# One explicit order of transfers for a residual-add layer norm: 16-row loads, stores ahead of the loads that follow them, finer last blocks

## Chip, cores and metric

The kernel runs on one core of a Trainium2 chip. The metric is device time in microseconds (us) of one execution; lower is better. A profiled execution gives a "span", about 1.3 us shorter than the device time of the same run. DVE is VectorE, ACT is ScalarE, POOL is GpSimd, SP is the sync engine, which issues all large transfers here. A core has 16 DMA engines, and every large transfer is spread over all of them (128 data packets, which the packet records show as 16 chains of 8).

"Row" means below one row of the 512 numbers *in each of the 128 partitions*: 128 x 2 KB = 256 KB. The problem has 128 such rows. So x16+16 is the load of rows 16 to 31 of x, 4 MB; r is the residual and o the output.

## The reference

```python
# x, residual: (16, 1024, 512) float32; gamma ones, beta zeros; eps 1e-5
z = x + residual
mean = np.mean(z, axis=-1, keepdims=True)
var = np.var(z, axis=-1, keepdims=True)
return (gamma * (z - mean) / np.sqrt(var + eps) + beta).astype(np.float32)
```

Each number of x and residual is read once and each of the output written once: 100.66 MB in all, and no order of transfers changes that.

## The kernel before

x is loaded into a ring of 64 rows (zbuf), the residual into a ring of 32 rows (rbuf). POOL adds the residual in place, ACT takes the mean and the sum of squares of each row in groups of four, DVE normalizes in place, and zbuf is stored. SP issues every transfer in one queue, and waits on semaphores where a ring is not yet free. The order of issue comes from a rule:

```python
X_CHUNKS = [8] * 15 + [4, 4]           # R_CHUNKS is the same
OUT_CHUNKS = [16] * 7 + [8, 4, 4]
Z_ROWS = 64; R_ROWS = 32; STORE_LAG = 40; ADD = 8
# ... (cut)
for c, (lo, n) in enumerate(loads_x):
    asked = lo + n
    while stored < asked - Z_ROWS:                 # the ring slot's old rows must be stored
        o = next(i for i, b in enumerate(stores) if b[0] == stored)
        nc.sync.wait_ge(so[o], 16)
        stored += stores[o][1]
    move(part(zbuf, Z_ROWS, lo, n), dram(xf, lo, n), sx[c])
    while todo_r and todo_r[0][1][0] + todo_r[0][1][1] <= asked:
        rc, (rlo, rn) = todo_r.pop(0)
        wait_rows(s_add, "add", rlo + rn - R_ROWS) # the residual slot must have been added
        move(part(rbuf, R_ROWS, rlo, rn), dram(rf, rlo, rn), sr[rc])
    while todo_o and (todo_o[0][1][0] + todo_o[0][1][1] <= asked - STORE_LAG or asked == total):
        oc, (olo, on) = todo_o.pop(0)
        wait_rows(s_out, "out", olo + on)          # the rows must be normalized
        move(dram(of, olo, on), part(zbuf, Z_ROWS, olo, on), so[oc])
# ... (cut: POOL adds each residual chunk, in pieces of ADD rows; ACT and DVE work in groups of 4 rows)
```

## Time and profile before

| | before |
|---|---|
| device time, median (lowest to highest) of the first 3 runs | 239.17 us (239.12 to 239.27) |
| transfers by SP; data packets per DMA engine | 44; 352 |
| share of the DMA engines' time that the packets took | 99.3% |
| ACT, DVE, POOL busy | 78%, 74%, 60% |

These lines are from the page of the kernel before: the span, the engines' busy time with shares, DMA's busy tenths and GB/s in 40 equal slices, the packets, the queue's share of 16 engines, and the chain of work that ended last, by engine and by line.

```profile
span 237.9 us, 1484 instructions
...
PE 3.7 (2%) x4; PEld 1.2 (0%) x4; DVE 177.2 (74%) x290; ACT 185.5 (78%) x545; POOL 142.2 (60%) x21
...
DMA  8999999999999999999999999999999999999996
GB/s 309 441 433 421 433 433 433 419 427 441 421 438 419 438 427 424 468 441 386 427 433 435 441 413 433 430 449 430 413 430 419 457 441 383 455 435 430 421 417 287
DMA packets 6341, 100.68 MB, mean 423 GB/s; under 512 B 706, under 2 KB 706, under 8 KB 708
...
q1 hardware_dynamic: 6336, 100.67, 99.3%
...
DMA 49%; ACT 24%; POOL 11%; DVE 5%; issue 4%; SPq 1%; ACTq 1%; DVEq 0%; POOLq 0%
DMA rbuf<-in_residual_dram 36%; ACT junk_s L211 14%; DMA out_dram<-zbuf 13%; POOL zbuf L181 11%; ACT junk_m L201 10%; DVE zbuf L239 3%; DVE zbuf L251 3%; SPq L138 1%; ACTq L201 1%; DVEq L239 0%; ACT std L220 0%; DVE rstd L248 0%; ACTq L192 0%; ACTq L198 0%; DVEq L231 0%
...
```

How to read them: the DMA row is 9 (90% or more) in every slice but the two at the ends, and the queue's packets took 99.3% of the engines' time. No compute engine is above 78%. The core is bound by its DMA engines, and it moved 423 GB/s over the whole span. The Trainium skill ("HBM Reference", Specifications (TRN2)) says of a core that streams alone that it measures about 425 GB/s, "bounded by its 16 DMA engines"; this trace agrees.

The next two fences show, first, the SP queue's own waits in the kernel before (what waited, for what, us in total, times, longest); second, POOL's adds, with their idle time after the bar.

```profile
engine line waited for: us in total, times, longest us
SPq L138 <- DMA out_dram<-zbuf: 110.5, 4, 29.1
SPq L138 <- DVE zbuf L251: 64.7, 6, 29.0
SPq L138 <- POOL zbuf L181: 33.8, 3, 15.8
...
```

```profile
...
L181 POOL TENSOR_TENSOR zbuf<-zbuf,rbuf 128x4096 f32<-128x4096 f32 (+1 forms) x17 | 142.0, 8353 | 70.6 <-DMA rbuf<-in_residual_dram 70.6
...
```

SP waited 209 us of a span of 238, and POOL 70.6 us for residual loads. Neither is a cost in itself. SP's part of the timeline shows it around the first store:

```profile
...
50.50 0.35 SPq L138 DMA_DIRECT2D out_dram<-zbuf  x1
50.89 0.43 SPq L138 DMA_DIRECT2D zbuf<-in_x_dram  x1
51.37 0.43 SPq L138 DMA_DIRECT2D rbuf<-in_residual_dram  x1
80.94 0.33 SPq L138 DMA_DIRECT2D zbuf<-in_x_dram  x1
...
```

SP stood still from 51.8 to 80.9 us, waiting for the store asked for at 50.5 to land. But an x load and a residual load had been put behind that store. The packet records show the store's last packets ending at 80.0 us at the median engine, and those two loads then keeping it busy until 89.8. SP had asked for the next x load at 80.9, 8.9 us in time.

The trace also holds one record for each packet. One transfer makes 8 data packets on each engine, one for each partition; its packet is as long as its rows in that partition: 8 KB for 4 rows, 16 KB for 8, 32 KB for 16. In the kernel before, packets took at the median 309, 613 and 1213 ns. So 16 KB cost a little more than half of 32 KB.

### The profile page before, as it was taken

The page shows a single profiled execution, that of the slowest core. Times are in us where ns is not written, and L with a number is a line of the kernel's source. Part 1 is how long each engine was busy: PE and PEld are TensorE (multiplying, and loading weights), DVE is VectorE, ACT ScalarE, POOL GpSimd, SP SyncE. Part 2 cuts the span into 40 slices and gives each one's busy share as a digit, 9 for nine tenths or more (in the row PEclk, how much of TensorE's full clock was granted, in tenths as well). Part 3 has the DMA queues.
Part 4 walks back from the last instruction along what each step waited for, and adds up shares of the span by engine and source line. Part 5 has one row for each costly group of instructions (what it writes and reads, how often), then busy time and mean ns, then how long its engine had stood idle before and what let it go on. Part 6 is the DMA issues. An engine that isn't in the chain of part 4 may idle for free.

```text
span 237.9 us, 1484 instructions
## 1 busy us (share of the span) xinstructions
PE 3.7 (2%) x4; PEld 1.2 (0%) x4; DVE 177.2 (74%) x290; ACT 185.5 (78%) x545; POOL 142.2 (60%) x21
## 2 busy tenths in 40 slices
PE   0600000000000000000000000000000000000000
PEld 0100000000000000000000000000000000000000
DVE  0000498989898989898989898963989549898950
ACT  2003999999999999999999999739996399999600
POOL 0098988989889407893078930889209892770000
DMA  8999999999999999999999999999999999999996
GB/s 309 441 433 421 433 433 433 419 427 441 421 438 419 438 427 424 468 441 386 427 433 435 441 413 433 430 449 430 413 430 419 457 441 383 455 435 430 421 417 287
DMA packets 6341, 100.68 MB, mean 423 GB/s; under 512 B 706, under 2 KB 706, under 8 KB 708
## 3 DMA queue, kind: packets, MB, share of 16 engines
q1 hardware_dynamic: 6336, 100.67, 99.3%
q14 instruction: 1, 0.01, 0.0%
q10 hardware_dynamic: 4, 0.00, 0.0%
HBM read 67.11 MB, written 33.55 MB: 423 GB/s over the span
## 4 chain that ended last, share of the span: by engine, by line
DMA 49%; ACT 24%; POOL 11%; DVE 5%; issue 4%; SPq 1%; ACTq 1%; DVEq 0%; POOLq 0%
DMA rbuf<-in_residual_dram 36%; ACT junk_s L211 14%; DMA out_dram<-zbuf 13%; POOL zbuf L181 11%; ACT junk_m L201 10%; DVE zbuf L239 3%; DVE zbuf L251 3%; SPq L138 1%; ACTq L201 1%; DVEq L239 0%; ACT std L220 0%; DVE rstd L248 0%; ACTq L192 0%; ACTq L198 0%; DVEq L231 0%
## 5 line engine op out<-in xcount | busy, mean ns | idle before, releaser
L181 POOL TENSOR_TENSOR zbuf<-zbuf,rbuf 128x4096 f32<-128x4096 f32 (+1 forms) x17 | 142.0, 8353 | 70.6 <-DMA rbuf<-in_residual_dram 70.6
L239 DVE SCALAR_TENSOR_TENSOR zbuf<-zbuf,nm,gamma_p 128x512 f32 x128 | 87.1, 742 | 48.7 <-ACT junk_s L211 48.7
L201 ACT ACTIVATE junk_m<-zbuf 128x512 f32 x128 | 74.8, 585 | 31.5 <-POOL zbuf L181 29.1
L211 ACT ACTIVATE junk_s<-zbuf,nm 128x512 f32 x128 | 88.9, 695 | 1.0
L251 DVE SCALAR_TENSOR_TENSOR zbuf<-zbuf,rstd,beta_p 128x512 f32 x128 | 87.1, 743 | 1.1
L211 ACT ACTIVATION_READ_ACCUMULATOR junk_s<-zbuf,nm 128x1 f32 x128 | 23.9, 187 | 0.0
L201 ACT ACTIVATION_READ_ACCUMULATOR junk_m<-zbuf 128x1 f32 x128 | 23.9, 186 | 0.0
L220 ACT ACTIVATE std<-ssq,eps_t 128x4 f32<-128x4 f32 x32 | 9.5, 297 | 3.0
L248 DVE RECIPROCAL rstd<-std 128x4 f32<-128x4 f32 x32 | 5.4, 170 | 0.0
L189 ACT ACT_TABLE_LOAD x1 | 1.3, 1283 | 2.7 <-PEq L56 2.7
L123 PE MATMUL gamma_p<-gb_row,ones 1*128 1x512 f32 x2 | 2.0, 1118 | 7.2 <-DMA gb_row<-in_gamma_dram 7.2
L123 PE MATMUL beta_p<-gb_row,ones 1*128 1x512 f32 x2 | 1.9, 1052 | 0.0
L118 DVE MEMSET ones<- 1x128 f32 x1 | 0.2, 165 | 2.0 <-PEq L56 2.0
L123 PEld LDWEIGHTS beta_p<-gb_row,ones 1*128 1x128 f32 x2 | 0.7, 328 | 1.0 <-issue 0.5
L123 PEld LDWEIGHTS gamma_p<-gb_row,ones 1*128 1x128 f32 x2 | 0.5, 308 | 7.2 <-issue 7.2
L287 POOL MEMSET const-float32-0.0<- 128x1 f32 x1 | 0.1, 99 | 0.2 <-issue 0.2
L287 POOL MEMSET const-bfloat16-1.0<- 128x1 bf16 x1 | 0.1, 102 | 0.0
L287 POOL MEMSET const-uint8-127<- 128x1 uint8 x1 | 0.1, 102 | 0.0
L287 POOL MEMSET const-float32-1.0<- 128x1 f32 x1 | 0.1, 99 | 0.0
L119 DVE MEMSET eps_t<- 128x1 f32 x1 | 0.1, 59 | 0.0
## 6 DMA issues: line engine op xcount, KB each, us to landing
zbuf<-in_x_dram SPq DMA_DIRECT2D x15, 2048.0 KB, 32.9
rbuf<-in_residual_dram SPq DMA_DIRECT2D x15, 2048.0 KB, 30.1
out_dram<-zbuf SPq DMA_DIRECT2D x7, 4096.0 KB, 28.5
zbuf<-in_x_dram SPq DMA_DIRECT2D x2, 1024.0 KB, 32.5
rbuf<-in_residual_dram SPq DMA_DIRECT2D x2, 1024.0 KB, 34.5
out_dram<-zbuf SPq DMA_DIRECT2D x1, 2048.0 KB, 15.7
out_dram<-zbuf SPq DMA_DIRECT2D x2, 1024.0 KB, 10.4
gb_row<-in_gamma_dram ACTq DMA_DIRECT2D x1, 2.0 KB
```

Source lines behind the costliest of these rows:

```text
L118: nc.vector.memset(ones[:, :], 1.0).then_inc(s_const, 1)
L123: nc.tensor.matmul(dest[:, :], ones[:, :], gb_row[:, k * D : (k + 1) * D], start=True, stop=True).then_inc(s_pe, 1)
L138: i = nc.sync.dma_start(out=out, in_=in_).then_inc(s, 16)
L181: nc.gpsimd.tensor_tensor(out=z, in0=z, in1=part(rbuf, R_ROWS, a, an), op=ALU.add).then_inc(s_add, an)
L189: act.preload_act_table_set("sqrt_and_others")
L201: i = act.activation(out=junk_m[k][:, :], in_=zk[k], func=ACT.Identity, scale=-inv_d, accum_out=nm[j][:, k : k + 1],)
L211: i = act.activation(out=junk_s[k][:, :], in_=zk[k], func=ACT.Square, bias=nm[j][:, k : k + 1], accum_out=ssq[j][:, k : k + 1],)
L220: act.activation(out=std[j][:, :], in_=ssq[j][:, :], func=ACT.Sqrt, bias=eps_t[:, 0:1], scale=inv_d,).then_inc(s_std, TURN)
L239: dve.scalar_tensor_tensor(out=zk[k], in0=zk[k], scalar=nm[j][:, k : k + 1], in1=gamma_p[:, :], op0=ALU.add, op1=ALU.mult,)
L248: dve.reciprocal(out=rstd[j][:, :], in_=std[j][:, :]).then_inc(s_dve, TURN)
L251: i = dve.scalar_tensor_tensor(out=zk[k], in0=zk[k], scalar=rstd[j][:, k : k + 1], in1=beta_p[:, :], op0=ALU.mult, op1=ALU.add,)
L287: nc = _bacc.Bacc("TRN2", target_bir_lowering=False, num_devices=1)
```

## The change

The intent: one list of transfers in place of the rule. Loads take 16 rows where they can, in 32 KB packets; each store is put ahead of the residual and x loads that follow it; the last blocks are finer than 16 rows (x in 8 rows, the last store in 12 and 4), though not finer than in the kernel before, which ends with x loads of 4 and 4 rows and stores of 8, 4 and 4; adds take 4, 4 and 8 rows of each block, so that ACT can start sooner.

```diff
-X_CHUNKS = [8] * 15 + [4, 4]
-R_CHUNKS = [8] * 15 + [4, 4]
-OUT_CHUNKS = [16] * 7 + [8, 4, 4]
+BLOCK = 16
-STORE_LAG = 40
-ADD = 8
+PLAN = """
+x0+8 r0+8 x8+8 r8+8 x16+16 r16+16 x32+16 r32+16
+x48+16 r48+16 o0+16 r64+16 x64+16 o16+16 r80+16 x80+16
+o32+16 r96+16 x96+8 x104+8 o48+16 r112+16 x112+8 x120+8
+o64+16 o80+16 o96+16 o112+12 o124+4
+"""
+ADDS = [4, 4, 8] * 7 + [4] * 4
 # ... (cut: parsing of PLAN; the DRAM view takes blocks of BLOCK rows)
+    for kind, lo, n in moves:
+        if kind == "x":
+            while gone < len(stores) and stores[gone][0] < lo + n - Z_ROWS:
+                nc.sync.wait_ge(so[gone], 16)
+                gone += 1
+            move(part(zbuf, Z_ROWS, lo, n), dram(xf, lo, n), sx[loads_x.index((lo, n))])
+        elif kind == "r":
+            wait_rows(s_add, "add", lo + n - R_ROWS)
+            move(part(rbuf, R_ROWS, lo, n), dram(rf, lo, n), sr[loads_r.index((lo, n))])
+        else:
+            wait_rows(s_out, "out", lo + n)
+            move(dram(of, lo, n), part(zbuf, Z_ROWS, lo, n), so[stores.index((lo, n))])
 # ... (cut: the loop by rule goes; POOL waits for the loads that each piece of ADDS needs)
```

ACT's and DVE's code and the bytes moved stay the same.

More of the change, by code (lines that the diff above doesn't have):

```diff
@@ L56, with of_kind @@
     tc.compile()
-    def spans(sizes):
-        assert sum(sizes) == total
-        return [(sum(sizes[:c]), n) for c, n in enumerate(sizes)]
-    blocks = spans(OUT_CHUNKS)
+    moves = []
+    for word in PLAN.split():
+        kind, (lo, n) = word[0], map(int, word[1:].split("+"))
+        assert lo // BLOCK == (lo + n - 1) // BLOCK
+        moves.append((kind, lo, n))
+    def of_kind(kind):
+        found = [(lo, n) for k, lo, n in moves if k == kind]
+        assert sum(n for _, n in found) == total
+        return found
     def dram(t, lo, n):
-        b0, bn = next(b for b in blocks if b[0] <= lo and lo + n <= b[0] + b[1])
-        v = t[P * b0 : P * (b0 + bn), :].rearrange("(p j) d -> p j d", p=P)
+        b0 = lo - lo % BLOCK
+        v = t[P * b0 : P * (b0 + BLOCK), :].rearrange("(p j) d -> p j d", p=P)
         return v[:, lo - b0 : lo - b0 + n, :].rearrange("p a b -> p (a b)")
@@ L92, in sem @@
         return s
-    loads_x, loads_r, stores = spans(X_CHUNKS), spans(R_CHUNKS), blocks
+    loads_x, loads_r, stores = of_kind("x"), of_kind("r"), of_kind("o")
     sx = [sem(f"sx{c}") for c in range(len(loads_x))]
@@ L125 @@
         ).then_inc(s_pe, 1)
-    todo_r, todo_o = list(enumerate(loads_r)), list(enumerate(stores))
     seen = {"add": 0, "out": 0}
@@ L140, in move @@
             first.append(i.ins)
-    stored = 0
-    for c, (lo, n) in enumerate(loads_x):
-        asked = lo + n
-        while stored < asked - Z_ROWS:
-            o = next(i for i, b in enumerate(stores) if b[0] == stored)
-            assert all(o != t[0] for t in todo_o)
-            nc.sync.wait_ge(so[o], 16)
-            stored += stores[o][1]
-        move(part(zbuf, Z_ROWS, lo, n), dram(xf, lo, n), sx[c])
-        while todo_r and todo_r[0][1][0] + todo_r[0][1][1] <= asked:
-            rc, (rlo, rn) = todo_r.pop(0)
-            wait_rows(s_add, "add", rlo + rn - R_ROWS)
-            move(part(rbuf, R_ROWS, rlo, rn), dram(rf, rlo, rn), sr[rc])
-        while todo_o and (
-            todo_o[0][1][0] + todo_o[0][1][1] <= asked - STORE_LAG or asked == total
-        ):
-            oc, (olo, on) = todo_o.pop(0)
-            wait_rows(s_out, "out", olo + on)
-            move(dram(of, olo, on), part(zbuf, Z_ROWS, olo, on), so[oc])
-    for o, (lo, n) in enumerate(stores[:-1]):
-        if lo >= stored:
-            nc.sync.wait_ge(so[o], 16)
+    gone = 0
+    for kind, lo, n in moves:
[10 more added lines that the diff above has]
+            move(dram(of, lo, n), part(zbuf, Z_ROWS, lo, n), so[stores.index((lo, n))])
+    for o in range(gone, len(stores) - 1):
+        nc.sync.wait_ge(so[o], 16)
     nc.sync.sem_clear(range(nums[0], nums[-1]))
@@ L169 @@
     nc.sync.sem_clear(range(nums[-1], nums[-1] + 1))
-    for c, (lo, n) in enumerate(loads_x):
-        nc.gpsimd.wait_ge(sx[c], 16)
-        for rc, (rlo, rn) in enumerate(loads_r):
-            if lo <= rlo < lo + n:
-                assert rlo + rn <= lo + n
-                nc.gpsimd.wait_ge(sr[rc], 16)
-                for a in range(rlo, rlo + rn, ADD):
-                    an = min(ADD, rlo + rn - a)
-                    z = part(zbuf, Z_ROWS, a, an)
-                    nc.gpsimd.tensor_tensor(
-                        out=z, in0=z, in1=part(rbuf, R_ROWS, a, an), op=ALU.add
-                    ).then_inc(s_add, an)
+    landed = {"x": 0, "r": 0}
+    lo = 0
+    for n in ADDS:
+        for key, loads, s in (("x", loads_x, sx), ("r", loads_r, sr)):
+            while landed[key] < len(loads) and loads[landed[key]][0] < lo + n:
+                nc.gpsimd.wait_ge(s[landed[key]], 16)
+                landed[key] += 1
+        z = part(zbuf, Z_ROWS, lo, n)
+        nc.gpsimd.tensor_tensor(
+            out=z, in0=z, in1=part(rbuf, R_ROWS, lo, n), op=ALU.add
+        ).then_inc(s_add, n)
+        lo += n
+    assert lo == total
     act = nc.scalar
```

## The prediction

> **What bounds the kernel now.** The DMA engines. The page's row of DMA busy tenths is 9 in all slices but the first and last, and its part on DMA queues gives q1 99.3% of the 16 engines' span, at 423 GB/s. The trace's packet records, laid out by engine, show no hole in the middle: first packet about 1.1 us into the span, then back to back (largest hole 0.34 us, on one engine), most engines ending near 236.15 us, and about 1.75 us of receipt and semaphores after. ACT (78%), DVE (74%) and POOL (60%) are not the limit. The sync queue's 110.5 us of waiting for stores, and POOL's 70.6 us for the residual, look like what the change attacks, but earlier transfers fill the DMA engines meanwhile, so this waiting costs nothing. The chain of waits names residual and store transfers because they stand in one full queue.
>
> The Trainium skill ("DMA: Bandwidth & Descriptors", Specifications) gives a fabric ceiling of 435 GB/s. The trace agrees: 32 KB packets of 1213 ns on 16 engines are 432 GB/s. 100.67 MB at 435 GB/s is 231.4 us; with the two ends about 234.3, so there is hardly 2% to win.
>
> **What the change does.** Bytes, DVE and ACT work stay. Transfers fall from 44 to 29, each 8 packets per DMA engine, so packets per engine from 352 to 232. Start to start, before's packets took 309 ns (8 KB), 613.6 (16 KB), 1211 (32 KB): two of 16 KB cost 16 ns more than one of 32 KB.
> Before: 31x8 of 16 KB (152.2) + 7x8 of 32 KB (67.8) + 6x8 of 8 KB (14.8) = 234.8 us; measured about 235.0.
> After: 19x8 of 32 KB (184.1) + 8x8 of 16 KB (39.3) + 8 of 24 KB (7.3, interpolated) + 8 of 8 KB (2.5) = 233.1 us. Gain 1.7 us, if 32 KB loads run as the 32 KB stores do. I take off a little.
>
> POOL has 25 adds in place of 17; two 4-row adds cost 9.06 us, one of 8 rows 8.87. ACT can start near 17 us instead of 21.3. Both off the critical path.
>
> **Does the queue stay fed?** By hand, from 0.613 us per row of transfer, 4.5/8.9 us adds, 5.9 us per 4 rows of ACT: r32 is asked for near 30 us with queued work until 49; r48 and o0 near 58 with work until 69; from x64 on each x load waits for the store 64 rows earlier, with one 16-row residual load (9.8 us) queued behind that store: a margin near 8 us. Loads end near 197; stores o64, o80, o96 hold the queue until 226; rows 124 and 128 are ready near 218 and 224. No hole expected.
>
> **Predicted time.** 239.17 - 1.5 = 237.7 us; 8 in 10 within 237.1 to 238.9. Faster by over 2%: 0.01; within 2%: 0.97; slower by over 2%: 0.02.
>
> **What the profile would show.** Right: about 4,200 packets in place of 6,341; busy tenths still 9 throughout; about 426 GB/s; the sync queue's and POOL's waits still large; last packet to end still near 1.75 us. Wrong: slices below 9 in 90-180 us (an x load asked for too late) or 224-230 us (last rows late), or 32 KB load packets slower than 1213 ns.
>
> **What would make it wrong.** 32 KB load packets much slower or faster than the stores; stores that land over 8 us after their last packet, a hole at every x load; the last 16 rows computed later than reckoned.

## The result and the profile after

| | before | after |
|---|---|---|
| device time, median (lowest to highest), 5 runs each | 239.27 us (239.12 to 239.43) | 238.07 us (238.04 to 238.31) |
| transfers by SP; data packets per DMA engine | 44; 352 | 29; 232 |
| packet time per DMA engine | 235.90 us | 234.80 us |

The ratio is 0.9955, 95% interval 0.9943 to 0.9967: 0.45% faster, well inside 2%, and clear of noise. "Packet time per engine" is the summed duration of all data packets divided by 16. Within a transfer, the records of one engine overlap by 3 to 4 ns, so this sum counts a little time twice: 1.2 us per engine before, 0.8 after.

The same lines of the page, after:

```profile
span 236.9 us, 1471 instructions
...
PE 3.7 (2%) x4; PEld 1.2 (0%) x4; DVE 177.2 (75%) x290; ACT 185.5 (78%) x545; POOL 143.0 (60%) x29
...
DMA  8999999999999999999999999999999999999996
GB/s 310 443 432 426 426 443 443 443 443 443 426 415 398 443 443 443 426 420 409 431 437 443 443 443 432 420 407 429 443 437 437 409 432 448 437 420 437 426 430 285
DMA packets 4181, 100.68 MB, mean 425 GB/s; under 512 B 466, under 2 KB 466, under 8 KB 468
...
q1 hardware_dynamic: 4176, 100.67, 99.2%
...
DMA 71%; POOL 9%; ACT 9%; DVE 2%; issue 2%; SPq 1%; ACTq 0%; DVEq 0%; POOLq 0%
DMA out_dram<-zbuf 49%; DMA rbuf<-in_residual_dram 16%; POOL zbuf L180 9%; DMA zbuf<-in_x_dram 6%; ACT junk_s L212 5%; ACT junk_m L202 4%; SPq L146 1%; DVE zbuf L240 1%; DVE zbuf L252 1%; ACTq L202 0%; DVEq L240 0%; ACT std L221 0%; DVE rstd L249 0%; ACTq L193 0%; POOLq L177 0%
...
```

The DMA row has not changed, there are 4181 packets in place of 6341, and the span is 1.0 us shorter. The chain of work now names stores for 49% where it named residual loads for 36%; in both kernels it only tells which member of one full queue something happened to wait for. SP's own waits and POOL's adds, after:

```profile
engine line waited for: us in total, times, longest us
SPq L146 <- POOL zbuf L180: 94.0, 6, 27.6
SPq L146 <- DMA out_dram<-zbuf: 74.0, 4, 21.0
SPq L146 <- DVE zbuf L252: 46.0, 3, 22.0
...
```

```profile
...
L180 POOL TENSOR_TENSOR zbuf<-zbuf,rbuf 128x2048 f32<-128x2048 f32 (+1 forms) x25 | 142.8, 5740 | 67.6 <-DMA zbuf<-in_x_dram 40.8
...
```

SP's waits sum to 214 us (209 before), and POOL's idle time fell from 70.6 to 67.6 us; POOL now waits for x loads more than for residual loads. All this moved, and none of it is where the 1 us came from. SP's timeline after, around the first store:

```profile
...
59.78 0.43 SPq L146 DMA_DIRECT2D out_dram<-zbuf  x1
78.83 0.33 SPq L146 DMA_DIRECT2D rbuf<-in_residual_dram  x1
90.61 0.33 SPq L146 DMA_DIRECT2D zbuf<-in_x_dram  x1
...
```

x64 is asked for at 90.6 us, when the store o0 has landed; at that moment the residual load r64 is in transfer, and x64's first packet starts at 99.3 at the median engine. The margin is 8.7 us, about as before (8.9).

One thing appears in the packet records that was not there before. At 76 to 79 us, in the last packets of r48, the load ahead of the first store, nearly every engine has slow packets: up to 465 ns over the usual 1213, in sum 0.37 us per engine. If one counts only packets more than 60 ns over the usual time of their size, the excess per engine is 0.69 us before (0.61 of it in the first 2 us) and 1.10 us after. So the shorter packet list saved 1.10 + 0.41 = 1.5 us of summed packet time, and 0.4 us was given back. Another 0.4 us of the 1.5 is only overlap of records that went away (1.2 us before, 0.8 after): from its first packet to its last, the mean engine took 234.9 us before and 234.2 after.

### The profile page after: what moved, and what is told of

Its sections match the earlier page's. It is cut to its first block, busy times and chain, and to the rows that moved or that the text cites. A ratio compares the mean times of both kernels' runs of the same rounds, so it can differ in the third digit from the quotient of the medians.

```text
span 236.9 us, 1471 instructions
## 1 busy us (share of the span) xinstructions
PE 3.7 (2%) x4; PEld 1.2 (0%) x4; DVE 177.2 (75%) x290; ACT 185.5 (78%) x545; POOL 143.0 (60%) x29
## 2 busy tenths in 40 slices
DMA packets 4181, 100.68 MB, mean 425 GB/s; under 512 B 466, under 2 KB 466, under 8 KB 468
## 3 DMA queue, kind: packets, MB, share of 16 engines
q1 hardware_dynamic: 4176, 100.67, 99.2%
## 4 chain that ended last, share of the span: by engine, by line
DMA 71%; POOL 9%; ACT 9%; DVE 2%; issue 2%; SPq 1%; ACTq 0%; DVEq 0%; POOLq 0%
DMA out_dram<-zbuf 49%; DMA rbuf<-in_residual_dram 16%; POOL zbuf L180 9%; DMA zbuf<-in_x_dram 6%; ACT junk_s L212 5%; ACT junk_m L202 4%; SPq L146 1%; DVE zbuf L240 1%; DVE zbuf L252 1%; ACTq L202 0%; DVEq L240 0%; ACT std L221 0%; DVE rstd L249 0%; ACTq L193 0%; POOLq L177 0%
## 5 line engine op out<-in xcount | busy, mean ns | idle before, releaser
L180 POOL TENSOR_TENSOR zbuf<-zbuf,rbuf 128x2048 f32<-128x2048 f32 (+1 forms) x25 | 142.8, 5740 | 67.6 <-DMA zbuf<-in_x_dram 40.8
## 6 DMA issues: line engine op xcount, KB each, us to landing
zbuf<-in_x_dram SPq DMA_DIRECT2D x6, 2048.0 KB, 14.9
```

The costliest lines, as they stand in the source:

```text
L180: nc.gpsimd.tensor_tensor(out=z, in0=z, in1=part(rbuf, R_ROWS, lo, n), op=ALU.add).then_inc(s_add, n)
```

## The experiments

Theory P: the gain is packet overhead only; order matters only in that the queue must never run empty. Rival O: the order of transfers (stores ahead, fewer or shorter waits) is itself worth the time. Runs of one batch share the chip and the runs of the kernel before.

### The changed kernel again

No edit.

> The changed kernel again, so that it stands on the same chip as the next three. Both theories: about 238.1 us, about 1.1 us below the kernel before. Its first profile held one stall of about 0.4 us on all 16 DMA engines near 77 us; if that was chance, this profile shows no such stall, and a span of about 236.7 us.

Measured: 238.26 us (238.08 to 238.51), ratio to before 0.9962 (0.9948 to 0.9976). The stall near 77 us was there again, 0.43 us per engine, and a second small one at 194 us (0.29). The first is no chance; the expectation of a clean profile was wrong.

### Its order, with 8-row loads

```diff
-x0+8 r0+8 x8+8 r8+8 x16+16 r16+16 x32+16 r32+16
+x0+8 r0+8 x8+8 r8+8 x16+8 x24+8 r16+8 r24+8 x32+8 x40+8 r32+8 r40+8
 # ... (all later 16-row loads alike; stores unchanged)
```

> The changed kernel's order, with each 16-row load cut into two of 8 rows (41 transfers, 328 data packets per DMA engine in place of 232). Packet theory (the gain is packet overhead, about 9 to 14 ns for each packet more): slower than the changed kernel by 0.9 to 1.3 us, about 239.1 us. Order theory (the gain is the order of transfers): as the changed kernel, 238.1 us.

Measured: 239.00 us (238.92 to 239.08), ratio to before 0.9994 (0.998 to 1.0007). The changed order, the stores ahead, the finer last blocks and the 4-row adds are all in this kernel, and with 8-row loads together they are worth nothing that can be told from zero. Rival O falls. From its page:

```profile
span 237.7 us, 1488 instructions
...
DMA packets 5909, 100.68 MB, mean 424 GB/s; under 512 B 658, under 2 KB 658, under 8 KB 660
...
q1 hardware_dynamic: 5904, 100.67, 99.3%
...
```

### Its order, with every transfer in pieces of 4 rows

```diff
-x0+8 r0+8 x8+8 r8+8 x16+16 r16+16 ...
+x0+4 x4+4 r0+4 r4+4 x8+4 x12+4 r8+4 r12+4 x16+4 x20+4 x24+4 x28+4 ...
 # ... (all loads and stores alike: 96 transfers)
```

> The changed kernel's order, with every transfer cut into pieces of 4 rows (96 transfers, 768 packets of 8 KB per engine). Packet theory: 768 packets at 306 to 309 ns are 235.3 to 237.3 us where the changed kernel has 233.1, so 2 to 5 us slower than the changed kernel, 240.5 to 243 us. Order theory: 238.1 us, or faster, since waits end on smaller pieces.

Measured: 242.79 us (242.54 to 242.88), ratio to before 1.0148 (1.0134 to 1.0162). From its page:

```profile
span 241.5 us, 1564 instructions
...
DMA packets 13831, 100.70 MB, mean 417 GB/s; under 512 B 1538, under 2 KB 1538, under 8 KB 1540
...
q1 hardware_dynamic: 13824, 100.67, 99.6%
...
```

The engines are even "busier" than before, 99.6%, and the kernel is slower: a busy DMA engine is not one at its best. The three kernels of this batch are a dose and a response, by their means: 232 packets per engine, 238.25 us; 328, 239.00 us; 768, 242.73 us. That is 0.75 us for 96 packets and 3.72 us for 440, so 7.9 and 8.5 ns for each packet more. The kernel before has 352 packets: 24 more than the second, and 239.00 + 24 x 8.5 ns gives 239.2; it measured 239.13. One line runs through four kernels, three with the changed order and one with the old; that is the strongest evidence for theory P.

The slope of that line is not the cost of one packet, however. In the 4-row kernel one engine ended 2.3 us after the median one (241.0 and 238.7 us), in the repeat of the changed kernel 0.8 us after it (236.5 and 235.7), so 1.6 of the 4.5 us between the two profiles come from one late engine; and the 232-packet kernel has the stall, which the other two lack. From start to start, without each kernel's first transfer, packets took 309 ns (8 KB, in the 4-row kernel), 611 (16 KB) and 1212 (32 KB; both in the kernel before): 10 ns for each packet more from 32 to 16 KB, 6 ns from 16 to 8 KB.

Two rivals go along with packet size in these runs. The packet records of the kernel before speak against both. Number of transfers: where a new transfer begins, the next packet starts 6 to 9 ns later than within one, so 15 transfers fewer are worth about 0.1 us (an estimate from these two numbers). Addresses: most 8-row loads read half of each partition's 32 KB in a 16-row block, but x112 and r112 have an 8-row block to themselves and read it whole, and their packets took 614 and 615 ns, like those of the other later 8-row loads (611 to 615).

### The old rule with 16-row loads, nothing else changed

```diff
-X_CHUNKS = [8] * 15 + [4, 4]
-R_CHUNKS = [8] * 15 + [4, 4]
+X_CHUNKS = [8, 8] + [16] * 6 + [8, 4, 4]
+R_CHUNKS = [8, 8] + [16] * 6 + [8, 4, 4]
```

> The kernel before with 16-row loads and nothing else changed: by its rule each store from the first on is now asked for just before the x load that waits for it. Queue theory: four holes of about 2 us, near 246 to 248 us, so larger loads alone are a loss and the order must come with them. If larger loads are all that counts: 238.3 us.

Measured: 252.18 us (251.78 to 252.47), ratio 1.0543. Its page's span and DMA row:

```profile
span 251.1 us, 1466 instructions
...
DMA  8999999999999979999699995999997999999998
...
```

The holes are where they were expected, one before each of x64, x80, x96 and x112, but they cost 13 us in place of 8. Why is taken up at the next run.

### The changed kernel with its stores behind the residual loads

```diff
-x48+16 r48+16 o0+16 r64+16 x64+16 o16+16 r80+16 x80+16
+x48+16 r48+16 r64+16 o0+16 x64+16 r80+16 o16+16 x80+16
 # ... (o32 and o48 alike)
```

> The changed kernel with each store from o0 to o48 moved behind the residual load that followed it, so that nothing is queued behind the store for whose landing the next x load waits. Theory that the order matters only in that it keeps the queue from running empty: four holes of about 2 us (0.8 us from the last packet to the next ask, 1.2 us from the ask to the first packet), 246 to 248 us, and a slice below 9 tenths at each. Theory that the queue has enough in it in any order: 238.1 us.

Measured: 253.18 us (253.08 to 253.60), ratio 1.059. From its page:

```profile
span 251.8 us, 1471 instructions
...
DMA  8999999999999999699996999969999799999998
GB/s 328 422 429 487 416 416 416 427 479 427 416 416 364 453 349 416 250 422 474 354 416 250 448 458 344 416 250 437 479 333 437 268 419 375 422 437 448 432 411 350
DMA packets 4181, 100.68 MB, mean 400 GB/s; under 512 B 466, under 2 KB 466, under 8 KB 468
...
q1 hardware_dynamic: 4176, 100.67, 96.5%
...
```

The bytes and packets are the same as in the changed kernel; the queue's share fell from 99.2% to 96.5%, and the DMA row dips at each store. SP's timeline at the first one, and the window of that hole (us; each engine's busy time; granted clock, DMA share, GB/s):

```profile
...
78.86 0.33 SPq L146 DMA_DIRECT2D rbuf<-in_residual_dram  x1
79.23 0.43 SPq L146 DMA_DIRECT2D out_dram<-zbuf  x1
102.01 0.33 SPq L146 DMA_DIRECT2D zbuf<-in_x_dram  x1
...
```

```profile
...
101.00:104.00 3.00, 0.00 (x0) 0.00 (x0) 2.77 (x5) 2.88 (x11) 0.00 (x0) 1.00 0.62 175
...
```

The store o0 is asked for at 79.2, and x64, which needs its ring slot, next, with nothing queued between. The store's packets end at 101.1 us at the median engine and 101.7 at the last, SP asks for x64 at 102.0, and its first packet starts at 103.1 at the median engine. The hole is 2.0 us, as expected: 0.9 from the median last packet to the ask, 1.1 from the ask to the first packet. The five gaps (0.4 us before r64, then 1.7 to 2.0 us after each of the four stores, means over the engines) sum to 7.7 us per engine. The Trainium skill ("DMA: Bandwidth & Descriptors", Anatomy of one DMA) gives a fixed cost of about 2.0 us for a DMA, most of it completion, for another issue path; a cost of that size is what shows here once nothing hides it, but in other parts: 1.1 of the 2.0 us lie between the ask and the first packet, and of the 0.9 us before the ask 0.6 is the wait for the last engine.

The other half had not been foreseen. After each hole, packets were slow: in the first packets after the restart (0.64 to 0.69 us per engine, as much as the 0.69 us of this kernel's own start), and again at the end of the loads, just ahead of the next store (0.85 to 1.1 us per engine). By the count of packets over 60 ns late, the excess is 9.2 us per engine, against 1.5 in the repeat of the changed kernel. Gaps of 7.7 and 7.7 us of excess make 15.4 us, and the median engine does end 15.4 us later than in that repeat (251.1 and 235.7 us). The spans differ by 251.8 - 236.9 = 14.9, because the last engine ends 0.3 us after the median here and 0.8 us after it there. So the size that was wrong is settled: an empty queue costs not only its gap but about as much again in slow packets after it. What makes the packets ahead of the next store slow was not found.

So the order is worth a great deal in one sense: 16-row loads need it. With the old rule they cost 13 us; with the list they save 1.

### The old rule with 16-row loads and stores asked for 8 rows sooner

```diff
 # the chunk lists as in the old rule with 16-row loads above
-STORE_LAG = 40
+STORE_LAG = 32
```

> The kernel before with its own rule of order, x before residual, only with 16-row loads, and stores asked for 8 rows earlier so that there is still a load behind each store (32 transfers, 256 packets per engine). Packet theory: nearly all of the gain, about 238.3 us. Order theory: no gain, about 239.2 us.

Measured: 245.65 us (245.47 to 246.25), ratio 1.0279. Both expectations missed. From its page:

```profile
span 244.2 us, 1466 instructions
...
DMA  8999999999999999999999999999999999989574
...
q1 hardware_dynamic: 4608, 100.67, 96.5%
...
```

There is no hole at the x loads: the lag did what it was chosen for. The holes are in the last slices. With x96 and r96 as one transfer each, POOL could begin on row 96 only at 178.2 us, when all of r96 had landed; in the kernel before it began at 159.4, in the changed one at 163.4. ACT takes 5.9 us for four rows, so the last 32 rows take it 47 us, and the stores of the last blocks were asked for at 216.4, 228.4, 234.5 and 240.3 us, each after its predecessor had ended at the median engine. The gaps before them there are 1.1, 2.2, 1.2 and 3.3 us: 7.8 us, against 7.4 us between this kernel's time and the changed one's (238.26 in the same batch). So this run does not speak about packets or order in the middle; it shows the second thing that an order must do: bring the last rows in early enough. That is what the split of x96 and x112 in the list was meant for; that the split itself is needed is not shown. In the kernel with two pairs of transfers merged (below), x96 is one load of 16 rows in the changed order: POOL began on row 96 at 168.8 us, and no hole came of it.

### Adds of 8 rows

```diff
-ADDS = [4, 4, 8] * 7 + [4] * 4
+ADDS = [8] * 15 + [4, 4]       # first kernel
+ADDS = [8] * 14 + [4] * 4      # second kernel
```

> The changed kernel with adds of 8 rows and 4, 4 at the end, as the kernel before has them. If the adds are off the critical path: 238.1 us. Worked out from the changed kernel's trace: rows 112 to 119 would be added 4.4 us later, the store of 12 rows asked for near 225.3 us, when its predecessor ends at 225.6, and a hole of about 0.9 us before it: about 239.0 us.

> Adds of 8 rows up to row 112, and four of 4 rows at the end: if only the last block's adds matter, 238.1 us, as the changed kernel, although ACT starts 4.4 us later.

Measured, in one batch: 238.28 us (238.24 to 238.48) and 238.19 us (238.13 to 238.31), ratios to before 0.9963 and 0.9958, no difference that can be told from the changed kernel's. The adds are off the critical path, as predicted. But 0.9 us had been expected of the first: its hole before the store of 12 rows is there, 0.45 us at the median engine, yet its time did not follow. The reason is in the next run.

### The last block stored whole

```diff
-o64+16 o80+16 o96+16 o112+12 o124+4
+o64+16 o80+16 o96+16 o112+16
```

> The changed kernel with the last block stored as one of 16 rows, in place of 12 and 4. It can be asked for only when row 128 is ready, at 226.7 us, 1.1 us after the store before it has ended; with 1.2 us from the ask to the first packet and 9.7 us of transfer the last packet ends near 237.6 in place of 235.4: about 2.3 us slower than the changed kernel, 240.4 us. If the finer last blocks don't matter: 238.1 us or a little less.

Measured: 239.14 us (239.04 to 239.20), ratio 0.9999; 0.95 us slower than the second kernel of the same batch (238.19), not 2.3. The store was asked for at 226.5, the hole was 1.6 us, and the median engine's last packet ended at 237.2 (235.4 in the changed kernel), near enough to what was worked out. What had been overlooked is that the engines do not end together. In the changed kernel one engine ends at 236.4 us, 1.0 us after the median, and the execution ends 0.5 us after *that* one. A hole lets the late engine catch up: here the last engine ended at 237.3, only 0.1 us after the median. So a hole of up to about 1 us near the end is mostly swallowed by the late engine, and beyond that it counts. Storing the last block in two pieces is worth about 1 us here, which is as much as the whole change; but the kernel before has fine last blocks too, so this is no part of the gain over it.

### Two pairs of transfers merged

```diff
-BLOCK = 16
+BLOCK = 32
-o32+16 r96+16 x96+8 x104+8 ...   o64+16 o80+16 o96+16 ...
+o32+16 r96+16 x96+16 ...         o64+32 o96+16 ...
```

> The changed kernel with two pairs of transfers merged (x96 and x104; o64 and o80 in one store with packets of 64 KB): 27 transfers, at most 216 packets per engine. Packet theory: 16 packets fewer at 9 to 14 ns, 0.15 to 0.2 us faster than the changed kernel, about 237.9 us, hardly beyond the spread; if packets of 64 KB are cut in two by the hardware, half of that.

Measured: 238.54 us (238.16 to 238.72), ratio 0.9974 (0.996 to 0.9988). No gain. 64 KB packets are not cut in two (one record of 65,536 bytes, 2418 ns at the median, 8 ns under two of 32 KB), but the stall near 77 us was longer in this profile, 0.76 us per engine. (BLOCK = 32 also changes the DRAM addresses of the other transfers: each now covers part of a 32-row block. Their 32 KB packets still took 1213 ns at the median.)

### Where the stall at 77 us comes from

All six kernels above that have the changed kernel's order up to the first store, with 16-row loads (the old rule with nothing else changed is one of them; the changed kernel itself was profiled twice), show slow packets at the end of the load ahead of it, 0.30 to 0.76 us per engine; the kernel with the old rule and the lag of 32 shows it (0.58 us) at 58 us, where its first store stands. The three kernels with loads of 8 rows or less show under 0.02 us. Two runs exchange only the load just ahead of the first store:

```diff
 # first kernel: the changed kernel
-... x48+16 r48+16 o0+16 ...
+... x48+16 r48+8 r56+8 o0+16 ...
 # second kernel: the changed order with 8-row loads
-... x48+8 x56+8 r48+8 r56+8 o0+16 ...
+... x48+8 x56+8 r48+16 o0+16 ...
```

> The changed kernel with only the residual load just ahead of the first store, r48, cut into two of 8 rows. In every profile of the changed kernel and its near variants the last two 32 KB packets of that load are slow on nearly all engines, 0.34 to 0.48 us in all per engine; the kernels with 8-row loads show less than 0.02 us there. Theory that the stall comes of 32 KB load packets just ahead of the first store: no stall near 77 us, 0.4 us saved, 8 packets more (0.13 us), so about 0.2 to 0.3 us faster than the changed kernel, near 238.0 us. Theory that it comes of the earlier 16-row loads or of the moment: the stall stays, 238.3 us or 0.1 us more.

> The reverse: all loads in pieces of 8 rows, only r48 as one of 16 rows. Packet size just ahead of the first store: a stall of about 0.4 us appears near 77 us, and the time is 0.2 to 0.3 us above that of the kernel with all loads in 8 rows, 239.2 to 239.3 us. Otherwise: no stall, 8 packets fewer, 238.9 us.

Measured: 238.36 us (238.20 to 238.61), with the stall still there (0.45 us per engine), and 238.82 us (238.77 to 239.07), without it (0.02). The theory that it is the packet size just ahead of the store falls, by both. Up to the first store it goes with the 16-row loads earlier on. After a restart it does not need them: in the two kernels with holes, only 8-row loads stand between the last restart and the store o64, and the load just ahead of o64 still has 0.6 and 1.0 us of slow packets. What mechanism makes it is open.

## Why the prediction was right

- *Bound by the DMA engines, waits of SP and POOL cost nothing:* right. They shifted by tens of us between causes, and the kernel with the new order and 8-row loads took the time of the kernel before (0.9994).
- *Packets of 8, 16, 32 KB cost what their records say, so 1.7 us, of which 1.5 was kept:* right in mechanism, but two sizes in the sum were wrong. First, the 613.6 ns of a 16 KB packet is a mean over all 248 of them, and the slow packets of the kernel's start (0.7 us per engine) are spread over it; without the first transfer it is 611.1 ns. That start is in both kernels, so about 0.5 us of the 1.7 was not there to win (184 packets of 16 KB fewer, 2.7 ns each). Second, the stall at 77 us, about 0.4 us, is missing. 1.7 - 0.5 - 0.4 is 0.8 us, and that is what the median engine shows: its last packet ended at 236.15 us before and at 235.36 after. The net effect was 1.2 us by the medians, 1.1 by the ratio, 0.9 by the medians of the repeat's batch. It lies inside the range that was stated, but below the 1.5 us; the little that was taken off was a guess.
- *The queue stays fed:* right, and closely. r32 was asked for at 31.0 us (about 30 predicted), r48 and o0 at 59.4 and 59.8 (58), loads ended at 196.5 (197), the last two stores were asked for at 220.9 and 226.7 (218 and 224). The margin of the x loads was 8.6 to 8.8 us (8). The margin at the end was 4.8 us for the store of 12 rows and 6.2 us for the last, thinner than the x loads'.
- *Adds off the critical path:* right, by the two kernels with 8-row adds.
- *About 1.75 us from the last packet to the end, unchanged:* read at the median engine, it was 1.75 before and 1.6 after. The reading of it was incomplete: most of it is not receipt, but one engine that ends 1.2 us (before) and 1.0 us (after) later than the median. The prediction had no term for it: of the 1.0 us by which the span fell, 0.2 us is that this engine ended less late, and since it was 0.8 us late in the repeat of the same kernel, this may be chance. It also made two of the later expectations too large.
- *4,200 packets, 426 GB/s:* 4181 and 425.
- *Less than 2% to win:* right. The fabric ceiling of 435 GB/s in the Trainium skill ("DMA: Bandwidth & Descriptors", Specifications) and 32 KB packets at 432 GB/s left room for little more than the 1 us that came. The 231.4 and 234.3 us of the prediction are estimates from that page's figure.

## What to carry to other kernels

When the DMA engines are full from end to end, look at the packet records, not at who waits for whom: the time is the sum of the packets, and of what was tried here only fewer and longer packets, up to 32 KB, shortened it for the same bytes (64 KB brought nothing more). Larger transfers then need an order in which something always stands in the queue behind a store whose landing the next load waits for, and in which the last rows come in early; getting one of these wrong cost 7 to 15 us here, where getting all right won 1. Cost a hole by the slowest of the 16 engines, and expect slow packets after it.

## What the Trainium skill lacked or had wrong

- "DMA: Bandwidth & Descriptors", Rules for kernel authors, asks for 128 partitions and at least 1 MiB per DMA for maximum bandwidth. All large transfers here meet that, in every kernel, and the time still went from 238.3 to 242.8 us as packets went from mostly 32 KB to 8 KB, about 8 ns per packet.
- "DMA: Bandwidth & Descriptors", Why small descriptors are slow, tells of a fixed overhead per packet of about 3 cycles, with a descriptor of 256 B as its example. It says nothing of large ones: here two packets of 16 KB (613 ns each) still take 13 ns more than one of 32 KB (1213 ns; from start to start it is 10 ns), and one of 64 KB (2418 ns) only 8 ns less than two of 32 KB.
- "DMA: Bandwidth & Descriptors", Latency and other measured facts, gives about 600 ns to the first byte on this issue path, and does not say from where it counts. Here it fits from the end of the issue instruction: the first packet record began 0.6 us after it, at the start of the changed kernel (0.38 to 1.01 us) and with an empty queue (102.34 to 102.97 us in the kernel with its stores behind the residual loads). From the start of the instruction it was 1.0 us.
- No page has the cost of letting a full queue run empty under large loads: beside the 2 us of the gap, the two kernels with holes show 0.5 to 0.9 us of slow packets at each restart and 0.6 to 1.1 us ahead of the next store.
- No page has the stall of 0.30 to 0.76 us ahead of the first store, seen after 16-row loads and not after 8-row loads alone. Its cause is open.
- "DMA: Bandwidth & Descriptors", Latency and other measured facts, calls the DMA engines 7 and 15 usually slower, and guesses at a cause that only another issue path has. Here SP issued all large transfers, and still one of the 16 engines ended 1.0 to 1.2 us after the median one (before and after; 2.3 us in the 4-row kernel). The packet records kept do not say which engine it was.
